# One gating tile issued ahead of the last gates and values, and the phasor table mirrored by GpSimd, in a two-layer streaming encoder

## The chip, the cores and the metric

The kernel runs on one core of one Trainium2 chip. Its engines are named as in the profile: PE (TensorE; PEld is its weight load), DVE (VectorE), ACT (ScalarE), POOL (GpSimd) and SP (SyncE, which here issues transfers only). ACT and SP both issue DMA transfers; ACTq and SPq stand for those instructions. The metric is the device time of one execution in microseconds (us), as the median of several runs.

## The reference

One inference step of a two-layer encoder, for 2,064 prompt tokens (16 of them meta tokens) and 128 sample tokens, 2,192 columns in all, in float32. The even layer, on which the change falls, computes:

```
def even_layer(h, g, i, st, P, segments):
    u = rmsnorm(h, g)
    ua, za, xb, zb = jnp.split(u @ P['ev_w_in'][i], [W_A, 2 * W_A, 2 * W_A + W_B], axis=-1)
    ya, s_re, s_im = s5_mixer(ua, ...)        # diagonal complex state space model, then a GLU: y * sigmoid(y @ w_glu)
    yb, mc, mn, mm, mbuf = mlstm_mixer(xb, ...)
    gated = jnp.concatenate([ya * jax.nn.silu(za), yb * jax.nn.silu(zb)], axis=-1)
    h = h + gated @ P['ev_w_out'][i]
```

In `mlstm_mixer`, a causal convolution over four tokens and a SiLU of `xb` give `xc`; `q` and `k` come from `xc` and `v` from `xb` by one matrix per head (four heads of 256); the input and forget gates are a product of `q`, `k`, `v` with `w_if`; a chunked recurrence follows. `zb` is the gating path. The odd layer (retention and an RG-LRU) is not touched by the change.

## The kernel before

Every float32 operand of a large product is split into a high and a low part (`split`, `narrow`), ACT casting the high part and POOL or DVE subtracting it for the low one; a product is then three TensorE instructions (`mm3`, L123 to L125). Tensors lie in SBUF with features on the 128 partitions and tokens along the row; tokens come in six blocks of up to 384 columns, and two blocks make a third.

The program is written phase by phase, and a scheduler of the Tile framework, which follows a simulated timeline, places each instruction on its engine's list, within the data dependences. Each engine runs its list strictly in that order. DMA transfers are issued in the order of the issuing engine's list.

Three phases matter here. In `phase_in0`, the S5 columns of the in-projection are made (`uas`, stored to `d_ua` by ACT at L305; `zst`, stored to `d_za` at L285). While the blocks run, `s5_turns` builds a table of phasors (powers of a rotation; `s5tb`, real and imaginary part, 128 partitions x 8 groups x 129 angles) for each of four groups of heads, one behind the other in the same piece of memory: DVE fills the upper 64 angles by doubling (L733 to L742, up to 128x256 elements per instruction), then the lower 64 are the upper ones in reverse order, times 1 for the real and -1 for the imaginary part (L744), and the table is stored to `d_rot` (L745, 1,032 KB). The next table may begin when the store has landed. At the end of the phase the first weights of the next phase (`w_first`: the load `xt`, the high part `wfh`, the low part `wfl`) are split into a place of memory that the tables give up.

`phase_l0` makes the mLSTM's input (`isz` 0) and its gating path (`isz` 1) third by third. `mtile(third, m, isz)` is one tile of 128 features: it loads a weight tile `wr`, splits it (`wh`, `wl`), multiplies it with the two blocks `ub` of the third (48 matmuls, into the PSUM tile `pm`), and for `isz` 0 does the convolution and yields what is late about it (the gate products `pg` of L428). `values` (L440 to L457) makes one head's `v` with its weights `wv`, `wvh`, `wvl` (36 matmuls of 264 columns for the six token tiles of a third). `settle(late)` runs the gate products and values still held back; `gate_out` writes the gates to memory (`d_g`, L516, L517), and the mLSTM's own opening reads them back (`g_i`, L1014). `s5` is a generator whose pieces are set between the tiles; behind its last products (the GLU, PSUM tile `s5p`, operands `s5gh`, `s5gl`) `phase_mlstm` follows (`pa` and `pc` tiles), whose first part is opened by `m_open` ahead of the gating tiles of the last third.

Of the kernel before, what the change touches and what calls it, by code (L numbers as in the profile page):

```python
# [13 lines left out]
OP = mybir.AluOpType  # L14
# [9 lines left out]
KD = 8  # L24
# [13 lines left out]
def P(e, name, bufs=1, side=None):  # L38
    return e.tc.tile_pool(name=name, bufs=bufs, side=side, reuse_waits="tile")
# [16 lines left out]
def cls(e, *names):  # L56
    for n in names:
        e.cms.pop(n).__exit__(None, None, None)
# [156 lines left out]
def phase_in0(e):  # L215
# [6 lines left out]
    with P(e, "a_w") as wp, P(e, "a_sb", 2) as sb, PS(e, "a_ps") as ps:  # L222
# [37 lines left out]
        for i, bi in enumerate(seq):  # L260
# [29 lines left out]
            if i == 1:  # L290
                with P(e, "prep", side="right") as rp:
                    prep_ml(e, rp, ps)
                s5_open(e, ps)
                s5_turns(e)
                cls(e, "s5pp")
# [59 lines left out]
def phase_l0(e):  # L355

    nc, tc = e.nc, e.tc
# [75 lines left out]
    def quarters(ut):  # L433

        n = sum(x[2] for x in ut) // 4
        return [(n * i, n) for i in range(4)]

    def values(h, ut, tiles, parts):

        h0 = ut[0][1]  # L440
        wv = xp.tile([128, 2, 264], F32, name="wv1", bufs=1)
        nc.sync.dma_start(wv[:, :, 0:256], e.i["ml_wv"][0, h].rearrange("(k p) f -> p k f", p=128))
        nc.gpsimd.tensor_copy(wv[:, :, 256:264], e.gw[:, 1, 2 * h:2 * h + 2, :])
        wvh = xp.tile([128, 2, 264], F32R, name="wvh1", bufs=1)
        wvl = xp.tile([128, 2, 264], F32R, name="wvl1", bufs=1)
        split(nc, wvh, wvl, wv, fine=True)
        for c, nt, kind, row in tiles:
            pv = ps.tile([128, 264], F32, name="pm1", bufs=4)
            cc = slice(c - h0, c - h0 + nt)
            for k in range(2):  # L450
                mm3(nc, pv[:nt], (parts[k][0][:, cc], parts[k][1][:, cc]), (wvh[:, k, :], wvl[:, k, :]), k == 0, k == 1)
            vo = xp.tile([128, 264], F32, name="vo1", bufs=3)
            nc.scalar.copy(vo[:nt], pv[:nt])  # L453
            nc.scalar.dma_start(e.v[c:c + nt, 256 * h:256 * (h + 1)], vo[:nt, 0:256])
            slot = 0 if kind == "x_sample" else 1 + tile_index(c)
            g = e.ga[:nt, :, slot, :]
            nc.gpsimd.tensor_add(g, g, vo[:nt, 256:264].rearrange("p (a b) -> p a b", a=2))  # L457
# [4 lines left out]
    def reload(bi):  # L462
        blk, b0, n = blks[bi]
        pool = e.ub_pool if bi % 3 < 2 else sb
        t = e.ub[bi] = pool.tile([128, 2, KD, 384], F32R, name=f"ub{bi % 3}", bufs=1)
        for c, nt, kind, row in blk:
            ur = xp.tile([128, KD, 128], F32, name="ut1", bufs=4)[:, :, :nt]
            nc.sync.dma_start(ur, e.u[:, :, c:c + nt])
            split(nc, t[:, 0, :, c - b0:c - b0 + nt], t[:, 1, :, c - b0:c - b0 + nt], ur)

    steps = 0
    for third in range(3):
        ut = [(bi,) + blks[bi][1:] for bi in (2 * third, 2 * third + 1)]
        tiles = blks[2 * third][0] + blks[2 * third + 1][0]
        pg = ps.tile([104, 192], F32, name="pg1", bufs=1)
        parts = []

        due, early, late = [], [], []
        if third > 0:

            early = [mtile(third, 0, 0, ut, pg, parts),
                     mtile(third, third % 2 == 0, third % 2, ut, pg, parts)]
            for g in early:
                next(g)
            reload(2 * third + 1)
            e.s5.loaded = third == 2

        def settle(held):

            for g in held:  # L490
                g()
            for h in due:
                values(h, ut, tiles, parts[2 * h:2 * h + 2])
            due.clear()

        def tile(m, isz):

            held = list(late)
            late.clear()
            for _ in early.pop(0) if early else mtile(third, m, isz, ut, pg, parts):  # L500
                pass
            settle(held)
            if m % 2 and not isz:
                due.append(m // 2)
            nonlocal steps
            steps += 1
            if steps == 1:
                cls(e, "w_first")
            if steps > 2:
                next(s5g, None)  # L510

        def gate_out():
            go = xp.tile([128, 2, 264], F32, name="wv1", bufs=1).rearrange("p a b -> p (a b)")
            for i, (o, n) in enumerate(quarters(ut)):
                g = slice(32 * i, 32 * i + 8)
                nc.scalar.activation(go[g, :n], pg[g, :n], AF.Identity, bias=bif[g])  # L516
                nc.scalar.dma_start(e.g8[:, ut[0][1] + o:ut[0][1] + o + n], go[g, :n])  # L517

        if third < 2:
            for m in range(KD):  # L520
                tile(m, 0)
                tile(m, 1)
                if m == 4:
                    reload(2 * third + 2)
            gate_out()
        else:
            for m in range(KD):
                tile(m, 0)
            for _ in s5g:
                pass  # L530
            settle(late)
            gate_out()
            co = xp.tile([128, D], F32, name="ut1", bufs=4)
            for g in range(2):
                pt = ps.tile([128, 512], F32, name="s5p", bufs=3)
                for m in range(4):
                    nc.tensor.transpose(pt[:27, 128 * m:128 * (m + 1)], cs[:, 4 * g + m, :], e.ident)
                nc.vector.tensor_copy(co[:27, 512 * g:512 * (g + 1)], pt[:27])
            nc.scalar.dma_start(e.o["p_ml_conv"].rearrange("a b c d -> (a b c) d"), co[0:3])
            nc.scalar.dma_start(e.o["s_ml_conv"].rearrange("a b c d -> (a b c) d"), co[3:27])  # L540
            cls(e, "b_x")
            m_open(e, ps)
            for m in range(KD):
                tile(m, 1)
    cls(e, "b_ps", "b_sb", "ub")

# [9 lines left out]
def cmul(v, o_re, o_im, a, b, s1, s2):  # L556
    v.tensor_mul(s1, a[0], b[0])
    v.tensor_mul(s2, a[1], b[1])
    v.tensor_sub(o_re, s1, s2)
    v.tensor_mul(s1, a[0], b[1])  # L560
    v.tensor_mul(s2, a[1], b[0])
    v.tensor_add(o_im, s1, s2)
# [122 lines left out]
MID = PCH // 2  # L685
# [37 lines left out]
def s5_turns(e):  # L723

    nc, v = e.nc, e.nc.vector
    p = e.s5
    with P(e, "s5co", side="right") as sb:
        for g0 in range(0, G, 8):
            gs = slice(g0, g0 + 8)
            tb = sb.tile([128, 2, 8, PCH], F32, name="s5tb")  # L730
            t1 = sb.tile([128, 8, 32], F32, name="s5r1")
            t2 = sb.tile([128, 8, 32], F32, name="s5r2")
            v.memset(tb[:, 0, :, MID], 1.0)  # L733
            v.memset(tb[:, 1, :, MID], 0.0)
            v.tensor_copy(tb[:, :, :, MID + 1], p.pp[:, :, 0, gs])
            for j in range(ROT):
                k = 1 << j
                sh = [128, 8, k]
                pk = [p.pp[:, i, j, gs, None].to_broadcast(sh) for i in range(2)]
                new, old = slice(MID + 1 + k, MID + 1 + 2 * k), slice(MID + 1, MID + 1 + k)  # L740
                cmul(v, tb[:, 0, :, new], tb[:, 1, :, new], (tb[:, 0, :, old], tb[:, 1, :, old]), pk,
                     t1[:, :, :k], t2[:, :, :k])  # L742
            for i in range(2):
                nc.scalar.mul(tb[:, i, :, 0:MID][:, :, ::-1], tb[:, i, :, MID + 1:], 1.0 - 2 * i)  # L744
            nc.scalar.dma_start(e.rot[:, :, gs, :], tb)  # L745


def s5_u(e, sb, q):
# [1310 lines left out]


PHASES = [phase_in0, phase_l0, phase_mlstm, phase_out0, phase_in1, phase_ret]


# [68 lines left out]
```

## Time and profile before

| what | value |
|---|---|
| time of three runs | 3120.72, 3131.16 and 3130.14 us, median 3130.14 us |
| the profiled execution's own time | 3125.61 us |
| its span, first to last instruction | 3123.9 us (1.7 us lie around it) |
| mean granted TensorE clock | 0.983 of full speed |
| busy over the span | PE 96%, DVE 55%, ACT 34%, POOL 31% |

All times of the trace are microseconds from the start of the span. PE's 4% of idle time is not spread evenly: one piece of it stands between 247 and 271 us, where `phase_in0` goes over into `phase_l0`.

### The profile page before, as it was taken

How to read it: one execution, taken by the hardware profiler on the slowest of the kernel's cores; microseconds unless marked ns; L12 is line 12 of the kernel's file. 1: busy time of each engine (PE TensorE's matmuls, PEld its weight loads, DVE VectorE, ACT ScalarE, POOL GpSimd, SP SyncE). 2: the span in 40 equal slices, each digit the busy share in tenths (PEclk: the TensorE clock that was granted, in tenths of full speed). 3: DMA queues.
4: the chain of work that ended last, by engine and by line, in shares of the span. 5: the costliest groups of instructions: out<-in, count | busy, mean ns of one | idle time of the engine just before them, and what ended most of it. 6: DMA issues, size and time to landing. Idle time of an engine off the chain costs nothing.

```text
span 3123.9 us, 45398 instructions
## 1 busy us (share of the span) xinstructions
PE 2995.7 (96%) x17435; PEld 2709.9 (87%) x17435; DVE 1717.8 (55%) x3482; ACT 1062.8 (34%) x1868; POOL 970.9 (31%) x1152
## 2 busy tenths in 40 slices
PE   8996999998999899999999999999999999999999
PEld 8996998997988887767799999999998898888887
DVE  4275885554547885233356666766610026665664
ACT  4223343335244433211235555555521112211221
POOL 6104664546436654111102111111100014433432
PEclk9998999998989999999999999999999999999999
DMA  6437555557634545665541111111122158544442
GB/s 214 120 100 210 158 168 151 164 165 159 209 91 149 171 153 171 212 196 169 152 147 59 48 49 52 51 52 52 43 84 75 52 157 249 140 127 131 135 124 75
DMA packets 447299, 404.82 MB, mean 130 GB/s; under 512 B 43593, under 2 KB 392977, under 8 KB 447082
## 3 DMA queue, kind: packets, MB, share of 16 engines
q1 hardware_dynamic: 335340, 272.36, 30.6%
q10 hardware_dynamic: 111742, 129.56, 12.4%
q8 instruction: 137, 2.24, 0.3%
q14 instruction: 80, 0.66, 0.1%
HBM read 266.35 MB, written 135.49 MB: 129 GB/s over the span
## 4 chain that ended last, share of the span: by engine, by line
PE 60%; DVE 8%; DMA 3%; issue 1%; ACT 1%; POOL 0%; SPq 0%; DVEq 0%; ACTq 0%; POOLq 0%
PE p_pm L124 8%; PE p_pm L125 8%; PE p_pm L123 8%; PE r_pm L125 4%; PE r_pm L124 4%; PE r_pm L123 4%; PE pa L123 3%; PE pa L124 3%; PE pa L125 3%; DVE p_d L1714 1%; PE pn L1363 1%; PE pc L1366 1%; DMA m_rw<-d_grow 1%; PE r_o L1916 1%; DVE m_qs L1206 1%
## 5 line engine op out<-in xcount | busy, mean ns | idle before, releaser
L123 PE MATMUL p_pm<-pu,p_wh 128*128 128x384 f32 (+1 forms) x1568 | 512.1, 327 | 0.2 <-ACT pu L105 0.2
L124 PE MATMUL p_pm<-pu,p_wh 128*128 128x384 f32 (+1 forms) x1568 | 511.8, 327 | 0.0
L125 PE MATMUL p_pm<-pu,p_wl 128*128 128x384 f32 (+1 forms) x1568 | 511.3, 326 | 0.0
L123 PE MATMUL pm<-ub,wh 128*128 128x384 f32 (+1 forms) x1136 | 378.6, 334 | 1.6 <-ACT vo L453 1.6
L124 PE MATMUL pm<-ub,wh 128*128 128x384 f32 (+1 forms) x1136 | 377.6, 332 | 1.6 <-DVE ub L109 1.6
L125 PE MATMUL pm<-ub,wl 128*128 128x384 f32 (+1 forms) x1136 | 375.2, 332 | 0.0
L123 PEld LDWEIGHTS p_pm<-pu,p_wh 128*128 128x128 f32 x1568 | 294.2, 188 | 1.8 <-issue 1.2
L124 PEld LDWEIGHTS p_pm<-pu,p_wh 128*128 128x128 f32 x1568 | 294.5, 188 | 1.0 <-issue 0.8
L125 PEld LDWEIGHTS p_pm<-pu,p_wl 128*128 128x128 f32 x1568 | 294.4, 188 | 0.0
L118 POOL TENSOR_TENSOR wl<-wr,wh 128x256 fp32r<-128x256 f32 x188 | 174.7, 959 | 222.4 <-ACT wh L105 222.4
L123 PEld LDWEIGHTS pm<-ub,wh 128*128 128x128 f32 x1136 | 216.3, 191 | 6.6 <-issue 4.0
L124 PEld LDWEIGHTS pm<-ub,wh 128*128 128x128 f32 x1136 | 216.3, 190 | 3.0 <-DVE ub L109 2.1
L124 PE MATMUL r_pm<-rol,r_gh 128*128 128x512 f32 x544 | 217.7, 401 | 1.1 <-POOL rol L109 0.6
L123 PE MATMUL r_pm<-roh,r_gh 128*128 128x512 f32 x544 | 217.9, 401 | 0.8 <-ACT p_o L1624 0.8
L125 PE MATMUL r_pm<-roh,r_gl 128*128 128x512 f32 x544 | 217.0, 400 | 0.7 <-DVE r_gl L109 0.7
L125 PEld LDWEIGHTS pm<-ub,wl 128*128 128x128 f32 x1136 | 215.9, 190 | 1.7 <-issue 1.6
L109 POOL TENSOR_TENSOR p_wl<-p_wr,p_wh 128x1024 fp32r<-128x1024 f32 x34 | 82.1, 2417 | 384.1 <-ACT p_wh L105 373.1
L109 POOL TENSOR_TENSOR p_xcl<-p_xc,p_xch 128x384 fp32r<-128x384 f32 (+1 forms) x48 | 46.8, 974 | 244.7 <-ACT p_xch L105 208.1
L125 PEld LDWEIGHTS r_pm<-roh,r_gl 128*128 128x128 f32 x544 | 102.9, 189 | 22.6 <-DVE r_gl L109 1.2
L124 PEld LDWEIGHTS r_pm<-rol,r_gh 128*128 128x128 f32 x544 | 102.9, 189 | 21.6 <-POOL rol L109 1.0
L123 PEld LDWEIGHTS r_pm<-roh,r_gh 128*128 128x128 f32 x544 | 102.7, 189 | 21.7 <-ACT p_o L1624 1.2
L1714 DVE RECIPROCAL p_d<-p_d 128x384 f32<-128x384 f32 (+1 forms) x48 | 116.7, 2430 | 0.6
(732 smaller groups left out, 6821.6 us busy)
## 6 DMA issues: line engine op xcount, KB each, us to landing
wr<-in_ev_w_in_dram SPq DMA_DIRECT2D x47, 512.0 KB
p_wr<-in_od_w_in_dram SPq DMA_DIRECT2D x40, 512.0 KB
d_in<-p_o ACTq DMA_DIRECT2D x80, 192.0 KB
m_rw<-d_grow SPq DMA_DIRECT2D x18, 512.0 KB
s5u<-d_ua SPq DMA_DIRECT2D x32, 274.0 KB
d_v<-vo ACTq DMA_DIRECT2D x68, 128.0 KB
m_va<-d_v SPq DMA_DIRECT2D x17, 512.0 KB
d_h<-o_x ACTq DMA_DIRECT2D x17, 512.0 KB
```

What stands on the lines that cost most here:

```text
L109: (nc.gpsimd if pool else nc.vector).tensor_tensor(l, x, h, op=OP.subtract)
L118: nc.gpsimd.tensor_tensor(out[:, c], a[:, c], b[:, c], op=op)
L123: nc.tensor.matmul(out, a[0], b[0], start=start, stop=False, **kw)
L124: nc.tensor.matmul(out, a[0], b[1], start=False, stop=False, **kw)
L125: nc.tensor.matmul(out, a[1], b[0], start=False, stop=stop, **kw)
L1206: v.tensor_tensor(qs[:, 4 * j:4 * j + 4, :n].rearrange("p (h m) n -> p h m n", m=2), qt[j][:, :, cs].rearrange("p (h m) n -> p h m n", m=2 ...
L1363: nc.tensor.matmul(pn[:n], c.qs[:, 2 * h + k, :n], ct[h][:, k, :], start=False, stop=k == 1)
L1366: nc.tensor.matmul(pc, c.kw[:n, h, 128 * k:128 * (k + 1)], c.va[:n, h, :], start=True, stop=True)
L1714: v.reciprocal(d[:, :n], d[:, :n])
L1916: nc.tensor.matmul(po, qk[:, h, :], S[:, h, :], start=False, stop=True)
```

## The change

Two edits. First, in the last third of `phase_l0`, the gating tile m = 0 is issued behind S5's last piece but ahead of `settle(late)` and `gate_out()`; the later loop starts at m = 1. Second, the mirror of the phasor table goes from ACT to POOL (with the reading side reversed instead of the writing side), and its store goes from ACT's list to SP's.

```
@@ phase_l0, third == 2
             for _ in s5g:
                 pass
+
+            for _ in mtile(third, 0, 1, ut, pg, parts):
+                pass
             settle(late)
             gate_out()
...
             m_open(e, ps)
-            for m in range(KD):
+            for m in range(1, KD):
                 tile(m, 1)
@@ s5_turns
             for i in range(2):
-                nc.scalar.mul(tb[:, i, :, 0:MID][:, :, ::-1], tb[:, i, :, MID + 1:], 1.0 - 2 * i)
-            nc.scalar.dma_start(e.rot[:, :, gs, :], tb)
+                nc.gpsimd.tensor_scalar(tb[:, i, :, 0:MID], tb[:, i, :, MID + 1:][:, :, ::-1], 1.0 - 2 * i, None,
+                                        op0=OP.mult)
+            nc.sync.dma_start(e.rot[:, :, gs, :], tb)
```

Each table has two mirror instructions of 128 x 8 x 64 elements and one store. In the changed file the mirror is L747 and the store L749.

POOL's list, where `phase_in0` ends and `phase_l0` begins (L185 and L186 are the last steps of the norm, `wl` and `wvl` the low parts of weights); before:

```order
L185 TENSOR_SCALAR rs_83<-rs_83 128x1
L186 TENSOR_TENSOR rs_83<-rs_83,mhalf 128x1
L408 MEMSET xb_2604 128x3
L443 COPY wv_2931<-gw 128x2x8
L118 TENSOR_TENSOR wl_2676<-wr_2673,wh_2675 128x256 x4
L118 TENSOR_TENSOR wl_2743<-wr_2740,wh_2742 128x256 x4
L118 TENSOR_TENSOR wvl_2935<-wv_2931,wvh_2934 128x264 x2
L443 COPY wv_3501<-gw 128x2x8
```

and of the change:

```order
L186 TENSOR_TENSOR rs_83<-rs_83,mhalf 128x1
L747 TENSOR_SCALAR s5tb<-s5tb 128x8x64 x6
L408 MEMSET xb_2604 128x3
L443 COPY wv_2931<-gw 128x2x8
L118 TENSOR_TENSOR wl_2676<-wr_2673,wh_2675 128x256 x4
L118 TENSOR_TENSOR wl_2743<-wr_2740,wh_2742 128x256 x4
L118 TENSOR_TENSOR wvl_2935<-wv_2931,wvh_2934 128x264 x2
L747 TENSOR_SCALAR s5tb<-s5tb 128x8x64 x2
L443 COPY wv_3501<-gw 128x2x8
```

The mirrors of the first three tables stand ahead of everything of `phase_l0`; the two of the fourth table stand behind ten splits of its weights.

SP's list at the same place (`bif` is the gates' bias, `ut` a block of the normed input read back); before:

```order
L300 DMA xt<-in_ev_w_in_dram 128x8x128
L368 DMA bif<-in_ml_b_if_dram 8x1 x4
L380 DMA wr_2673<-in_ev_w_in_dram 128x8x128
L380 DMA wr_2740<-in_ev_w_in_dram 128x8x128
L442 DMA wv_2931<-in_ml_wv_dram 128x2x256
```

and of the change:

```order
L300 DMA xt<-in_ev_w_in_dram 128x8x128
L749 DMA d_rot<-s5tb 256x1x1032 x3
L368 DMA bif<-in_ml_b_if_dram 8x1 x4
L380 DMA wr_2673<-in_ev_w_in_dram 128x8x128
L380 DMA wr_2740<-in_ev_w_in_dram 128x8x128
L442 DMA wv_2931<-in_ml_wv_dram 128x2x256
```

Three stores of tables now stand ahead of the loads of `phase_l0`. The fourth follows further on in the same list (`s5u` and `s5rt` are what S5 reads first):

```order
L468 DMA ut_4950<-d_u 128x8x128
L380 DMA wr_3057<-in_ev_w_in_dram 128x8x128
L468 DMA ut_4954<-d_u 128x8x128
L442 DMA wv_3501<-in_ml_wv_dram 128x2x256
L468 DMA ut_5951<-d_u 128x8x128
L749 DMA d_rot<-s5tb 256x1x1032
L757 DMA s5u<-d_ua 128x548 x2
```

It stands behind thirteen large loads of `phase_l0`, the last two of which are `wv_3501` (256 KB) and `ut_5951` (512 KB); before, no store of a table was on this list.

PE's list in the last third, where S5's GLU is under way (`pm_8190` is a value tile of head 3, `pm_8188` the gating tile m = 0, `pg` the gates); before:

```order
L428 MATMUL pg_6552<-xc_7605,gw 8x192 x4
L123 MATMUL pm_8190<-wvh_8185,xbh_7599 128x264
L124 MATMUL pm_8190<-wvl_8186,xbh_7599 128x264
L125 MATMUL pm_8190<-wvh_8185,xbl_7601 128x264
L123 MATMUL pm_8201<-wvh_8185,xbh_7599 128x264
```

and of the change at the same place:

```order
L428 MATMUL pg_6552<-xc_7605,gw 8x192 x4
L123 MATMUL pm_8188<-ub_5950,wh_8180 128x384
L124 MATMUL pm_8188<-ub_5950,wh_8180 128x384
L125 MATMUL pm_8188<-ub_5950,wl_8181 128x384
L123 MATMUL pm_8188<-ub_5950,wh_8180 128x384
```

The gating tile has taken the values' place. They now follow some 340 rows later on the same list, towards the end of the GLU:

```order
L125 MATMUL s5p<-s5gh,ut_6790 128x272
L428 MATMUL pg_6552<-xc_7858,gw 8x192 x2
L123 MATMUL pm_8253<-wvh_8248,xbh_7599 128x264
L124 MATMUL pm_8253<-wvl_8249,xbh_7599 128x264
L125 MATMUL pm_8253<-wvh_8248,xbl_7601 128x264
```

The last gates and the first value tile of head 3 stand here behind nearly all of the GLU's products.

## Rows read from the trace of the kernel before

**Rows 1.** The page: span, and busy time of each engine.

```profile
span 3123.9 us, 45398 instructions
PE 2995.7 (96%) x17435; PEld 2709.9 (87%) x17435; DVE 1717.8 (55%) x3482; ACT 1062.8 (34%) x1868; POOL 970.9 (31%) x1152
```

**Rows 2.** Waits between 180 and 320 us: total, times, longest.

```profile
POOL wl L118 <- ACT wh L105: 25.1, 4, 16.9
...
DVE s5tb L733 <- DMA d_rot<-s5tb: 31.7, 3, 14.9
...
PE pm L123 <- ACT wfh L105: 23.5, 1, 23.5
```

**Rows 3.** Windows: PE, PEld, DVE, ACT, POOL busy, clock, DMA share, GB/s.

```profile
247.00:270.50 23.50, 0.01 (x1) 0.00 (x0) 12.12 (x43) 9.88 (x14) 6.94 (x8) 0.59 1.02 311
...
785.00:826.00 41.00, 38.59 (x288) 37.29 (x287) 22.24 (x27) 13.78 (x35) 14.25 (x31) 1.00 0.45 150
826.00:888.00 62.00, 60.31 (x350) 58.88 (x347) 26.96 (x63) 17.42 (x27) 21.61 (x26) 1.00 0.74 221
888.00:937.00 49.00, 44.51 (x265) 35.05 (x266) 24.20 (x71) 24.94 (x56) 18.90 (x24) 0.83 0.23 67
```

**Rows 4.** Timeline of ACT, 238.5 to 270 us: start, duration, what, idle before.

```profile
239.23 6.55 ACTq L305 DMA_DIRECT2D d_ua<-uas  x8
...
245.85 1.70 ACTq L305 DMA_DIRECT2D d_ua<-uas  x2
247.59 1.16 ACT L744 ACTIVATE s5tb<-s5tb 128x512 f32<-128x512 f32 x2 [1.28 <-issue]
248.79 0.52 ACTq L745 DMA_DIRECT2D d_rot<-s5tb  x1
...
261.91 0.64 ACT L744 ACTIVATE s5tb<-s5tb 128x512 f32<-128x512 f32 x1 [11.30 <-DVE s5tb L559]
...
264.05 0.52 ACTq L745 DMA_DIRECT2D d_rot<-s5tb  x1
...
269.45 1.04 ACT L105 CAST wfh<-xt 128x1024 fp32r<-128x1024 f32 x1 [1.12 <-DMA d_rot<-s5tb]
```

**Rows 5.** Timeline of DVE, 222 to 272 us.

```profile
238.86 0.42 DVE L562 TENSOR_TENSOR s5tb<-s5r,s5r 128x256 f32<-128x256 f32 x1
254.14 0.07 DVE L733 MEMSET s5tb<- 128x8 f32 x1 [14.86 <-DMA d_rot<-s5tb]
...
262.71 0.42 DVE L562 TENSOR_TENSOR s5tb<-s5r,s5r 128x256 f32<-128x256 f32 x1
266.47 4.98 DVE L109 TENSOR_TENSOR ub<-ut,ub 128x1024 fp32r<-128x1024 f32 x3 [3.34 <-ACT ub L105]
```

**Rows 6.** Timeline of POOL, 240 to 312 us.

```profile
263.56 8.48 POOL L118 TENSOR_TENSOR wl<-wr,wh 128x256 fp32r<-128x256 f32 x8 [16.90 <-ACT wh L105]
272.00 3.42 POOL L118 TENSOR_TENSOR wvl<-wv,wvh 128x264 fp32r<-128x264 f32 x2
```

**Rows 7.** Timeline of SP (transfers issued), 240 to 285 us.

```profile
245.78 4.04 SPq L368 DMA_DIRECT2D bif<-in_ml_b_if_dram  x4
250.27 1.89 SPq L380 DMA_DIRECT2D wr<-in_ev_w_in_dram  x2
...
254.99 7.30 SPq L468 DMA_DIRECT2D ut<-d_u  x4
```

**Rows 8.** Tile `wr`, 240 to 300 us: its splits, shortest, median, longest in ns.

```profile
L118 POOL TENSOR_TENSOR wl<-wr,wh x16: 722/734/1720, 263.6 to 299.4; 128x256 fp32r<-128x256 f32 x16
```

**Rows 9.** POOL's groups by form: busy, mean ns, idle before.

```profile
L1222 POOL TENSOR_SCALAR_AFFINE_SELECT m_w<-m_w 128x512 f32<-128x512 f32 x17 | 14.3, 840 | 27.2 <-ACT m_w L1221 27.2
```

**Rows 10.** Waits of PE between 762 and 830 us.

```profile
PE s5p L123 <- DVE s5gy L991: 2.8, 3, 1.4
```

**Rows 11.** Tiles `g_i` (800 to 960 us) and `acol` (870 to 900 us).

```profile
L1014 SPq DMA_DIRECT2D g_i<-d_g x1: 265/265/265, 833.0 to 833.0; - x1
...
L1221 ACT ACTIVATE m_w<-m_rw,acol x8: 290/346/401, 894.8 to 899.1; 16x16 f32<-16x16 f32 x4, 128x128 f32<-128x128 f32 x4
```

## The prediction

> **What bounds the kernel now.** The page comes first [rows 1]: PE is busy for 96% of the span, DVE for 55%, and the rest is far below. So the kernel is PE's work plus the places where PE stands still, and a change that adds no matmul and removes none, as this one, can only move the 4% of idle time (about 128 us of 3123.9). Where these places are is read next. Both edits touch places that can be looked at by themselves: the tables are built until about 270 us, and the moved tile runs between 762 and 888 us.
>
> The waits between 180 and 320 us [rows 2] show one large stop of PE, 23.5 us, for the cast of `wfh`. In the windows [rows 3] the same stretch, 247 to 270.5, has PE at nothing while the DMA engines are full (share 1.02, 311 GB/s). Who ends it is read in the timeline of ACT [rows 4]: the cast of `wfh` starts at 269.45, released by the store of the fourth table, issued at 264.05 and landed 5.4 us later. That cast writes into memory which the tables give up, so PE's restart (269.45 + 1.04, and the first matmul at 270.55 by the waits' end) hangs on the fourth table, and this is a chain back: store issue 264.05, mirror from 261.91, DVE's table from 254.14 to 263.13 [rows 5], released by the landing of the third store, issued 248.79, its mirror at 247.59. The third table itself was ready at 239.28 [rows 5]; its mirror came 8.3 us late because ACT was issuing ten `d_ua` stores from 239.23 to 247.55 [rows 4]. So the chain to PE's restart runs through just the instructions that the second edit moves.
>
> The stretch around the first edit looks different [rows 3]: PE is busy for 38.6 of 41 us in 785 to 826 and 60.3 of 62 in 826 to 888. Between 762 and 830 it waits 2.8 us in all, three times, for S5's own DVE chain [rows 10].
>
> **Edit 1, the gating tile ahead of the last gates and values.** PE's work is the same in both orders: the tile's 48 matmuls of 384 columns, at 60.3 / 350 = 0.17 us each [rows 3] 8.3 us, go forward past 36 value matmuls and some gates. What it could gain is idle time that it fills: at most the 2.8 us of [rows 10], and these are waits in the middle of the GLU, which other ready matmuls already fill in part; the tile replaces the values as filling. What it could cost is that something behind the gates gets late: they go to `d_g`, which is read at 833.0, while the columns made from them are first used by ACT at 894.8 [rows 11]. The gates move back by some 8 us into this slack of 60 us, in which PE has gating tiles to run until 888 [rows 3]. I take nothing, with -3 and +3 as bounds (the waits of [rows 10] gone, or as much again). Without that cover, had the columns been needed at once, it would be up to the tile's 8.3 us. The scheduler also sets the recurrence's first matmuls anew; in 888 to 937 PE idles 4.5 us of 49 [rows 3], which such a shift can move by a few us either way.
>
> **Edit 2, third table.** On POOL, which idles here, the mirror can start when the table is ready, 239.3. The operation isn't in the trace. The nearest row is POOL's one-input instruction of the same 128x512, 0.84 us [rows 9]; a bound from below is ACT's 0.6 [rows 4], from above 0.84 stretched as POOL's splits stretch (1720 / 734 [rows 8]), 2.0. I take 0.84, so two end at 241.0. The store does not go at once: in the built program SP waits ahead of it for the completion of an earlier `d_ua` store, the same family that releases `bif` at 245.78 [rows 7]. I take 245.0 (241.0 to 248.8 as ends). Landing took 254.14 - 248.79 = 5.35, so the third table is stored at 250.4, a gain of 3.7 us.
>
> **Fourth table.** DVE needed 263.13 - 254.14 = 9.0; it ends at 259.4. Now POOL's list decides: its two mirrors stand behind ten splits of `phase_l0`'s first weights. These were held in [rows 2, 6] by ACT's cast (idle 16.9 us before 263.56), which stood behind ACT's mirror. With the mirror gone from ACT, the casts start when the weights land: issued 250.27 and 1.89 long for two [rows 7], 1.05 MB at the 311 GB/s of this stretch [rows 3] 3.4 us if it were alone, so about 254.5 beside other traffic, and a cast of 128x1024 takes 1.04 [rows 4]. Splits from 255.5 (253.5 to 257.5). They took 8.48 + 3.42 = 11.9 us for the ten [rows 6], while DVE did splits of its own [rows 5]; now DVE builds the table and then does those splits at the same time, so I keep 11.9: POOL is free at 267.4, 8 us after the table is ready. The bounds are ten at the median, 7.3, and ten at the longest, 17.2 [rows 8]. Mirrors to 269.1, store issue and landing 5.4 to 274.5, cast 1.04, and PE restarts at 275.5 to 275.6 instead of 270.55: **+5.0 us**. The fourth store's place on SP costs nothing if the loads ahead of it have been issued by 269. I take it that they have: the `ut` among them need buffers that DVE's splits give back, until 271.45 before [rows 5], and these splits follow a table that now ends 3.7 us sooner.
>
> Work that stands behind the mirror on POOL: small copies and the splits of the next tiles, which PE needs only after the restart. SP's first loads, behind three stores, go out as before, since the wait for `d_ua` held them until 245.78 already. PE pays the 5 us in full, as it has no other waits of size up to 320 [rows 2].
>
> Sum: 3125.6 + 5.0 + 0 = 3130.6 for an execution like the profiled one. The median of the runs shown is 4.5 above that execution, so the forecast is 3135 against 3130.1.
>
> **Rivals.**
> *The queue of SP.* The fourth store waits on SP's transfers behind `wv_3501` and `ut_5951` (0.77 MB, or 1.3 MB with the `ut` before them). For it: the DMA engines are full there (share 1.02). At 311 GB/s [rows 3] that is 2.5 to 4.2 us more, +7.5 to +9.2: 3138 to 3139. Against it: ACT's store shared the same full engines and landed in 5.4 us.
> The Trainium skill, page "DMA: Bandwidth & Descriptors", section "Queues, rings and completion order", says that SP and ACT each own a row of rings and that each DMA engine takes a row's descriptors in order and alternates between rows by packets. By that rule a store on ACT's row overtakes SP's loads and one on SP's row can't, which is this rival. No row of before shows a store on SP behind loads.
>
> *POOL is quick.* Splits at the median pace from 253.5 end at 260.8, mirrors 262.5, store 267.9, restart 269.0: -1.6, so 3128.5. For it: half of the splits take 0.73 or less [rows 8]. Against it: DVE is at work for most of those 7 us.
>
> *The tile fills the gaps.* All of the 2.8 us in [rows 10] and part of the 4.5 idle us at 888 to 937 disappear, edit 2 stays at the low end: 3126 to 3128.
>
> *Slow end.* DVE's two-operand table instructions hold POOL's two-operand splits down all the time: splits from 257.5 at 1.72 end at 274.7, mirrors at 2.0 each 278.7, store 284.1 and with 4 us of queue 288.1, restart 289.1, +18.6: 3149. It decides for slower by over 0.5% from 1.43 us a split with the other terms at their ends (257.5 + 14.3 + 4.0 + 5.4 + 4.0 + 1.04 = 286.2, against 270.55: +15.6).
> The Trainium skill, "GPSIMD Engine Reference", section "8. Key points", has GpSimd share its ports into SBUF with VectorE and contend with VectorE instructions of two SBUF inputs. The trace agrees for VectorE's 128x1024 splits: 0.73 us grew to as much as 1.72 beside them [rows 5, 8]; no row shows it for the table's small ones.
>
> *The opening moves the recurrence.* The scheduler's new order at 888 to 937 loses as much as that stretch idles now or more, 5 to 8 us: 3140 to 3143.
>
> **Chances and range.** Forecast (+2 to +7) 0.42; SP's queue 0.20; quick POOL 0.13; gaps filled 0.09; slow end 0.07; recurrence 0.09. 0.5%, about what a measurement of this kernel can tell from no change, is 15.6 us. Nothing here gives 15.6 us less (two thirds of the 23.5 us stop would have to go), so faster gets 0.04. Slower takes the slow end and mishaps together, 0.09; same 0.87. The runs of before differ by 10 us among themselves, which goes into the range: from 3121 (quick POOL and a low run) to 3147 (close to the slow end).
>
> **What would show it.** In the profile after: the first mirrors on POOL at about 239 to 241 and the third store issued near 245; the fourth table's end on DVE near 259.4; ten splits on POOL from 255 to 267 with the mirrors directly behind; PE's wait for `wfh` 28.5 us instead of 23.5. If the wait is under 23, the splits were quick or the third store went far earlier. If the store's landing takes 8 us or more, it is SP's queue. If PE's idle time in 762 to 937 changes by over 3 us, edit 1 is not the zero that I take. The forecast is wrong if PE's restart is between these bounds and the time is not: then something outside of both places moved.

## The result and the profile after

The change made the kernel slower: 3143.82 us as the median of four runs, against 3128.39 for the kernel before beside them, a ratio of 1.0051 (95% interval 1.0034 to 1.0067), or +15.4 us. The forecast was 3135 with a range of 3121 to 3147. The sign was the one forecast. Of the 15.4 us, 9.6 came at the place and along the chain that were forecast, about twice the +5.0 of the sum; the rest came in a later stage that the sum had put at nothing. One run of `e12_two_more` below, 3546 us at a granted clock of 0.784, was in a slower state of the chip and is left out of its median.

The page of the changed kernel, first lines: PE does the same work as before [rows 1], 2992.6 us of it, in a span that is 18.6 us longer than that of the profile before.

```profile
span 3142.5 us, 45397 instructions
PE 2992.6 (95%) x17435; PEld 2706.5 (86%) x17435; DVE 1717.0 (55%) x3482; ACT 1058.5 (34%) x1860; POOL 982.4 (31%) x1160
```

The waits between 180 and 340 us (total, times, longest). PE's stop for `wfh` has grown from 23.5 [rows 2] to 34.1 us, and the cast itself now waits 13.3 us for the store of the table; before, it waited 1.12 [rows 4].

```profile
POOL s5tb L747 <- DVE s5tb L562: 66.9, 3, 34.9
...
PE pm L123 <- ACT wfh L105: 34.1, 1, 34.1
POOL wl L118 <- ACT wh L105: 28.2, 5, 13.5
...
ACT wfh L105 <- DMA d_rot<-s5tb: 13.3, 1, 13.3
...
DVE xd L415 <- DMA bif<-in_ml_b_if_dram: 10.5, 1, 10.5
```

The timeline of POOL over the same stretch shows the fourth table's mirrors where its list has them: behind ten splits, and 3.92 us long. The earlier pairs, in front of which POOL idles, take 3.14 to 3.15 us. The last line is the view of the tile `s5tb` on POOL: shortest, median and longest of the eight mirrors in ns. The shortest is the fourth table's second one, which no work of DVE overlaps; the longest is its first one, which runs beside a split of DVE's (`ub`, 1.76 us from 268.45). The first mirror of the three earlier pairs runs beside the last steps of DVE's table and takes 1.67 to 1.68 us.

```profile
202.62 3.15 POOL L747 TENSOR_SCALAR s5tb<-s5tb 128x512 f32<-128x512 f32 x2 [34.91 <-DVE s5tb L562]
...
240.86 3.14 POOL L747 TENSOR_SCALAR s5tb<-s5tb 128x512 f32<-128x512 f32 x2 [19.06 <-DVE s5tb L562]
...
259.05 6.71 POOL L118 TENSOR_TENSOR wl<-wr,wh 128x256 fp32r<-128x256 f32 x8 [13.51 <-ACT wh L105]
265.72 3.40 POOL L118 TENSOR_TENSOR wvl<-wv,wvh 128x264 fp32r<-128x264 f32 x2
269.10 3.92 POOL L747 TENSOR_SCALAR s5tb<-s5tb 128x512 f32<-128x512 f32 x2
...
L747 POOL TENSOR_SCALAR s5tb<-s5tb x8: 1488/1586/2465, 202.6 to 271.5; 128x512 f32<-128x512 f32 x8
```

The timeline of SP (transfers issued), of two stretches. The third store goes at 244.03 instead of 248.79, the fourth at 273.05 instead of 264.05 [rows 4].

```profile
244.03 0.51 SPq L749 DMA_DIRECT2D d_rot<-s5tb  x1
244.63 7.29 SPq L368 DMA_DIRECT2D bif<-in_ml_b_if_dram  x4
252.66 1.40 SPq L380 DMA_DIRECT2D wr<-in_ev_w_in_dram  x2
...
273.05 0.56 SPq L749 DMA_DIRECT2D d_rot<-s5tb  x1
```

The timeline of ACT. The cast of the first weight, which waits for its landing, starts only at 257.93, and the cast of `wfh` ends at 280.05, where PE starts again (280.11).

```profile
245.34 4.17 ACTq L305 DMA_DIRECT2D d_ua<-uas  x2
...
257.93 1.04 ACT L105 CAST wh<-wr 128x1024 fp32r<-128x1024 f32 x1 [7.11 <-DMA wr<-in_ev_w_in_dram]
...
279.01 1.04 ACT L105 CAST wfh<-xt 128x1024 fp32r<-128x1024 f32 x1 [13.28 <-DMA d_rot<-s5tb]
```

The timeline of DVE. The fourth table begins at 253.07, only 1.1 us earlier than before [rows 5], because a small copy (`xd`) now stands ahead of it on DVE's list and waits for transfers; and it ends at 265.2, 12.1 us later instead of 9.0. Its steps of 128x256, 0.42 us before [rows 5], take 0.83 to 0.95 while POOL splits beside them.

```profile
252.93 0.18 DVE L415 COPY xd<-pc 128x24 f32<-128x24 f32 x1 [10.54 <-DMA bif<-in_ml_b_if_dram]
253.07 0.07 DVE L736 MEMSET s5tb<- 128x8 f32 x1
...
264.35 0.83 DVE L565 TENSOR_TENSOR s5tb<-s5r,s5r 128x256 f32<-128x256 f32 x1
```

So the restart moved from 270.55 to 280.11, by 9.6 us. That leaves about 6 of the 15.4 us in the medians, and 9 of the 18.6 in the profiles, for something behind it.

### The profile page after: what moved, and what is told of

It is laid out like the page before. It is cut to its first block, busy times and chain, and to the rows that moved or that the text cites. A ratio compares the mean times of both kernels' runs of the same rounds, so it can differ in the third digit from the quotient of the medians.

```text
span 3142.5 us, 45397 instructions
## 1 busy us (share of the span) xinstructions
PE 2992.6 (95%) x17435; PEld 2706.5 (86%) x17435; DVE 1717.0 (55%) x3482; ACT 1058.5 (34%) x1860; POOL 982.4 (31%) x1160
## 4 chain that ended last, share of the span: by engine, by line
PE 61%; DVE 8%; DMA 2%; issue 1%; ACT 1%; POOL 1%; SPq 0%; ACTq 0%; DVEq 0%; POOLq 0%
PE p_pm L124 8%; PE p_pm L125 8%; PE p_pm L123 8%; PE r_pm L124 4%; PE r_pm L125 4%; PE r_pm L123 4%; PE pa L123 3%; PE pa L124 3%; PE pa L125 3%; PE pn L1367 1%; PE pc L1370 1%; DVE p_d L1718 1%; PE pa L1235 1%; DMA m_rw<-d_grow 1%; DVE p_xc L554 1%
```

## The experiments

Theory A was that the restart is all of it, theory B that the first edit adds something behind it, theory C that the stores on SP's list do the damage. Theory D came after the first runs: the scheduler writes a different list for the mLSTM's recurrence, far behind the edit. Each kernel was timed beside the kernel before on the same chip; "restart" is PE's first matmul with `wfh` in its profile, and "list" says how PE's list of the recurrence, as the traces have it, stands to that of before (apart from the tile that the first edit moves).

| kernel | edit | median and difference, us | ratio, 95% | restart, us | list |
|---|---|---|---|---|---|
| the change | both | 3143.82, +15.4 | 1.0034 to 1.0067 | 280.1 | as e2_table |
| e1_tile | first edit alone | 3124.22, -3.8 | 0.9978 to 1.0002 | 270.3 | before, but for 63 rows near its end |
| e2_table | second edit alone | 3142.09, +14.1 | 1.0033 to 1.0061 | 281.4 | other, some 600 rows |
| e3_pool_actq | mirror on POOL, store on ACT | 3142.40, +15.8 | 1.0041 to 1.0066 | 279.0 | as e2_table |
| e4_act_spq | mirror on ACT, store on SP | 3128.27, +0.2 | 0.9991 to 1.0009 | 271.6 | before |
| e5_dve_spq | mirror on DVE, store on SP | 3128.11, +0.2 | 0.9994 to 1.0011 | 270.5 | before |
| e7_hybrid | fourth table as before | 3132.11, +4.2 | 1.0000 to 1.0025 | 273.5 | before, but for some 110 rows near its end |
| e8_order | 3 mirrors more on ACT | 3138.99, +11.1 | 1.0021 to 1.0047 | 274.5 | as e2_table |
| e9_late | 28 mirrors more on ACT | 3144.93, +17.0 | 1.0043 to 1.0067 | 289.8 | before |
| e10_three_dve | DVE, fourth on ACT | 3130.38, +3.7 | 1.0000 to 1.0019 | 269.2 | before |
| e11_three_dve_tile | the same and first edit | 3124.78, -1.9 | 0.9984 to 1.0003 | 270.9 | as e1_tile |
| e12_two_more | e2_table, 2 mirrors more | 3138.25, +11.1 | 1.0021 to 1.0047 | 282.0 | as e1_tile |

**e0_before**, the kernel before unchanged, for a second profile of it.

> The kernel before, unchanged, as a second profile of it. Theory A (the time beyond PE's restart is a gather that runs at a different pace from one execution to the next): the last of the four activations on s5gy starts some 16 us after the first in the profile of before and 30.4 us in that of the change; here the figure lies anywhere between, and the span moves with it by up to 5 us against 3123.9. Theory B (the slower gather belongs to the change): the figure is 24.8 us as in the profile of before (741.99 - 717.23 = 24.8), and the span within 2 us of 3123.9.

Its span is 3127.6 us, its restart 270.7. The timeline of ACT has the four activations on S5's gathered output:

```profile
717.78 2.04 ACT L953 ACTIVATE s5gy<-s5gy 128x2192 f32<-128x2192 f32 x1
...
729.36 2.03 ACT L953 ACTIVATE s5gy<-s5gy 128x2192 f32<-128x2192 f32 x1 [7.19 <-DMA s5gy<-d_ys]
...
747.20 2.03 ACT L953 ACTIVATE s5gy<-s5gy 128x2192 f32<-128x2192 f32 x1
```

From first to last 29.4 us, where the first profile of the same kernel had 24.8 and the change's has 30.4. (The expectation's "16 us" for the first profile is a slip; 24.8, further on in it, is the figure.) So some 5 us of the difference between the two first profiles is this gather, which takes another time in another execution; the profile of before was an unusually quick one there. The comparisons below use e0_before.

**e1_tile and e2_table**, the two edits apart.

```
e1_tile   + for _ in mtile(third, 0, 1, ut, pg, parts): pass        (ahead of settle(late); later loop from 1)
e2_table  - nc.scalar.mul(...)         + nc.gpsimd.tensor_scalar(...)
          - nc.scalar.dma_start(...)   + nc.sync.dma_start(...)
```

> The first edit alone. Theory A (all of the loss is in the table's chain to PE's restart): restart near 270.5 us as before, time -3 to +2 us against the kernel before. Theory B (the moved tile changes loads and reads around S5's gather and costs the 5 to 6 us that the trace of the change loses between 700 and 762 us): restart near 270.5, but +3 to +6 us.

> The second edit alone. Theory A: PE's wait for wfh is 34 us and its restart at 280 us as in the changed kernel, +9 to +16 us against the kernel before, that is the whole of the change's loss. Theory B: restart at 280, +9 to +10 us and no more, the rest being the first edit's.

The second edit alone gives +14.1 us, the whole of the change's loss within the intervals; theory B fell. The first edit alone measured -3.8 us, in an interval (-6.9 to +0.6) that includes zero. But e2_table's restart is 10.8 us late, and theory A as it stood does not say where the rest went.

**e4_act_spq and e3_pool_actq**, one half of the second edit each.

```
e4_act_spq     mirror: nc.scalar.mul          store: nc.sync.dma_start
e3_pool_actq   mirror: nc.gpsimd.tensor_scalar  store: nc.scalar.dma_start
```

> The mirror stays on ACT, only the store goes to SP's list. Theory A (GpSimd's place behind ten splits and its 1.6 us per mirror make the restart late, the store's list does not): the fourth mirror at about 262, the fourth store right behind it (its place on SP's list is here ahead of the last input loads), restart at 269 to 272, time -3 to +3 us. Theory C (stores on SP's list delay the weight loads and collide with the last S5 stores, and this is what costs): wr issued at 252.5 instead of 250.3 us, restart 274 or later, +4 us or more.

> The second edit with the store left on ACT's list; the mirror on GpSimd. Theory A (GpSimd's mirrors, their place and price): the fourth mirrors again end at 270 to 273 us, the store lands 5.4 us later, restart at 278 to 281, and the recurrence has the second edit's list: +11 to +15 us. Theory C (the stores on SP's list hold up the loads): wr issued at 250 instead of 252.6, splits 2.5 us sooner, restart at 276 to 277, +9 us or less.

In the time, the store's list costs nothing that can be measured, and the mirror on POOL costs everything: theory C fell. (At the restart the store's list does show in one of them: in e2_table the store is issued at 272.76, 1.7 us behind its mirrors, because `wv` and `ut` stand ahead of it on SP's list, and lands 7.56 us later; in e3_pool_actq it goes at once and lands in 6.83, and the restart is 2.4 us sooner.) In e3_pool_actq `wr` was issued at 250.29 and not at 252.66, and yet the first cast of it, the first sign that it has landed, began at 257.80, as late as in the change:

```profile
257.80 1.04 ACT L105 CAST wh<-wr 128x1024 fp32r<-128x1024 f32 x1 [8.58 <-DMA wr<-in_ev_w_in_dram]
...
271.10 0.52 ACTq L746 DMA_DIRECT2D d_rot<-s5tb  x1
277.93 1.04 ACT L105 CAST wfh<-xt 128x1024 fp32r<-128x1024 f32 x1 [11.71 <-DMA d_rot<-s5tb]
```

**e7_hybrid**: POOL and SP for three tables, the fourth as before on ACT.

```
+ if g0 < 24: nc.gpsimd.tensor_scalar(...)   else: nc.scalar.mul(...)
+ (nc.sync if g0 < 24 else nc.scalar).dma_start(...)
```

> The second edit for the first three tables; the fourth keeps ACT for its mirror and its store. Theory A (what costs is the fourth mirror's place on GpSimd, behind ten splits, and its 2 us a piece there): table four ends at 262 to 263 as in the change, ACT's mirror by 264.5, store landed at 270, restart at 271 to 272, +0 to +2 us. Theory C (the three stores on SP's list cost): restart at 276 or later, +5 us or more.

Restart 273.5, 7.9 us sooner than e2_table's: the fourth table's mirror on POOL carries most of the late restart. What is left over the kernel before is seen on DVE: the fourth table began at 253.42 and its last step is this, with the mirror right behind it on ACT at 266.59:

```profile
253.42 0.07 DVE L733 MEMSET s5tb<- 128x8 f32 x1
...
265.71 0.84 DVE L562 TENSOR_TENSOR s5tb<-s5r,s5r 128x256 f32<-128x256 f32 x1
```

13.1 us for a table that took 9.0 [rows 5]: with ACT's casts no longer behind a mirror, POOL's splits start while the table is being made and hold DVE up.

**e8_order and e9_late**, the restart and the recurrence's list apart. A few mirrors more on ACT (they write the same values again) are enough for the scheduler to write PE's list of the recurrence exactly as e2_table has it; with 28 more, PE's list is exactly that of before.

```
e8_order   - for i in range(2):    + for i in [1] * (3 if g0 == 24 else 0) + [0, 1]:
e9_late    - for i in range(2):    + for i in [0, 1] * (15 if g0 == 24 else 1):
```

> The kernel before, with the second mirror of the fourth table done three times more on ACT. The restart is late by some 2 us (3 x 0.63), and this is enough that the scheduler writes PE's list of the mLSTM's recurrence, far behind, in just the order that it has with the second edit. Theory D (the loss behind the restart, some 4 us in the medians, is this other order): +5 to +7 us. Theory A (only the restart counts): +1.5 to +2.5 us.

> The kernel before, with the fourth table's mirrors done 28 times more on ACT; PE's list, the recurrence included, is the same as before. The restart is late by 17 to 18 us (28 x 0.63). If a late restart is paid in full and no more (theories A and D): +16 to +19 us. If what follows recovers some of it: less; if a late restart by itself makes later stages slower, as the second edit's +14 for a restart 10 us late could mean: +22 us or more.

e9_late is late by 19 us at the restart and costs 17.0: a late restart is paid about once, no more. e8_order is late by 4 us (not 2) and costs 11.1. So the list costs some 7 us in this pair of medians (2.7 to 10.8 by the interval), more than theory D expected. The waits of PE between 890 and 1270 us show it. In e0_before they sum to 33.0 us in ten rows, the first of which are:

```profile
PE pa L123 <- DVE m_g L1272: 17.3, 5, 3.5
PE pc L1366 <- DVE ct L1370: 4.6, 3, 1.8
PE pa L1269 <- DVE m_g L1272: 3.9, 2, 3.5
```

In e8_order 36.8 us in twelve rows, with a new one, for `m_yn`:

```profile
PE pa L123 <- DVE m_g L1272: 13.9, 4, 3.5
PE pc L1366 <- DVE ct L1370: 7.1, 4, 2.6
PE pa L1269 <- DVE m_g L1272: 4.4, 3, 3.5
PE pn L1361 <- ACT m_yn L1256: 3.9, 3, 1.6
```

And in the changed kernel 38.8 us, with the same pattern:

```profile
PE pa L123 <- DVE m_g L1276: 13.9, 4, 3.5
PE pc L1370 <- DVE ct L1374: 7.3, 5, 2.6
PE pn L1365 <- ACT m_yn L1260: 4.9, 3, 2.2
```

The windows of the whole stage, from the last matmul of `phase_l0`'s gating tiles to the first of the output projection, say the same. In order: e0_before, e5_dve_spq and e10_three_dve with the list of before, then e8_order and the change with the other (length; PE, PEld, DVE, ACT, POOL busy; clock; DMA share; GB/s).

```profile
893.00:1206.50 313.50, 280.40 (x1624) 241.56 (x1623) 246.74 (x732) 130.81 (x273) 177.92 (x215) 0.92 0.47 143
894.10:1203.00 308.90, 275.76 (x1623) 236.91 (x1623) 247.59 (x732) 130.60 (x273) 178.26 (x215) 0.94 0.47 145
889.70:1207.40 317.70, 282.48 (x1623) 243.75 (x1623) 246.30 (x732) 130.40 (x273) 177.08 (x215) 0.92 0.47 141
894.80:1213.50 318.70, 281.80 (x1623) 241.33 (x1623) 238.63 (x727) 129.55 (x272) 174.91 (x213) 0.93 0.45 137
900.00:1219.50 319.50, 280.53 (x1623) 241.02 (x1623) 238.69 (x726) 129.29 (x272) 174.69 (x213) 0.94 0.45 137
```

PE is idle for 33.1, 33.1 and 35.2 us in the first three, for 36.9 and 39.0 in the last two. Over all profiles the four kernels with the other list have 36.9 to 39.0 us, all the rest 32.2 to 35.2, and e9_late, with the latest restart, 33.1. So the order itself is worth 4 to 6 us of PE's idle time. The length of the stage is a weaker sign: PE's busy time for the same matmuls differs by 7 us between two executions with one list (275.8 at a granted clock of 0.94, 282.5 at 0.92).

**e12_two_more**: e2_table with the fourth table's second mirror done twice more on POOL, with which the list comes out almost as before.

```
- for i in range(2):    + for i in [1] * (2 if g0 == 24 else 0) + [0, 1]:
```

> The second edit, with the fourth table's second mirror done twice more on GpSimd. The restart is 3 to 4 us later still, at 284 to 285 us, but the scheduler's list of the recurrence is, but for eight short pieces near its end, that of before. Theory D (the second edit's list costs some 4 us behind the restart): +12 to +14 us, no more than the second edit alone. Theory A' (a restart late by 10 us costs 14 whatever the list): +17 to +18 us.

More work on the path, and 11.1 us lost instead of 14.1, about as much as the restart is late (11.4). The restart was less late than expected, because the store left right behind the last mirror and landed in 5.94 us, where e2_table's was held as said above; and two intervals of this width (6.6 to 14.7 and 10 to 19 us) overlap, so this run alone would decide little; the waits, 34.0 us without the row for `m_yn`, go with it.

**e5_dve_spq, e10_three_dve and e11_three_dve_tile**, versions that might beat both.

```
e5_dve_spq      v.tensor_scalar(...), nc.sync.dma_start(...) for all four tables
e10_three_dve   the same for three, nc.scalar.mul and nc.scalar.dma_start for the fourth
e11_three_dve_tile   e10_three_dve and the first edit
```

> The mirror on DVE, right behind each table, the store on SP's list (ahead of the last input loads); PE's list is that of before. A mirror of 128x512 is not in the trace for DVE; 0.3 to 0.6 us from its 0.42 for 128x256 with two inputs. Theory A: third store at about 244, table four from about 250 to 260, its store at 260 to 261, restart at 267 to 268, that is 2.5 to 3.5 us earlier than before: -2 to -4 us. Theory C (an early third store holds up the last S5 stores and with them everything on SP): restart at 271 or later, no gain.

> The first three tables' mirrors on DVE with their stores on SP's list, the fourth's on ACT ahead of the casts of the weights, with its store on ACT's list; PE's list is that of before. Theory A: the third store lands at 250 to 251 and table four, with no GpSimd split beside it, takes 9.0 us to 260; mirror on ACT to 261.3, store 262.4 (a cast stands between), landed 267.8, restart at 268.9, some 2 us earlier than before: -1 to -3 us. Theory C (an early third store costs as much as it gives): restart at 270.5 to 272, 0 to +2 us.

> The same with the first edit, and the recurrence's list as the first edit alone has it: the sum of the two, -4 to -8 us, if they do not touch each other; if the first edit's 4 us were chance, -1 to -3 us.

On DVE the mirror takes 0.42 us, and in e5_dve_spq the third table's second one was done at 237.5; its store still had to wait for the S5 stores. In e5_dve_spq the splits on POOL began at 258.38, beside the table, and the last mirror ended at 263.7; nothing was gained. In e10_three_dve the mirror on ACT stands ahead of the casts, the splits begin at 262.68, and the table is undisturbed; its last step:

```profile
251.75 0.07 DVE L733 MEMSET s5tb<- 128x8 f32 x1 [14.09 <-DMA d_rot<-s5tb]
...
260.57 0.43 DVE L562 TENSOR_TENSOR s5tb<-s5r,s5r 128x256 f32<-128x256 f32 x1
```

9.2 us, and the restart came 1.5 us sooner. But the time is +3.7 us (0 to +5.9), which the restart does not explain. Its profile has the excess in the recurrence, 4.2 us over e0_before's with the same list (2.1 idle, 2.1 busy, by the windows above); the cause is open. No version here is measurably faster than the kernel before; e1_tile and e11_three_dve_tile come nearest.

## Why the prediction was right in kind and too small

The measured time lies in the stated range, but the central case (+2 to +7, chance 0.42) did not come: the measured interval is +10.6 to +21. That 3143.8 lies under the 3147 is in part luck. The upper end was set for POOL's splits at their slowest; what filled it was a chain twice as late as summed, for other reasons, and a loss in the recurrence. Nor was 15.6 us the smallest change that can be told from none: the interval here is some 5 us to either side.

**The chain to the restart** was read rightly: third store early, fourth mirrors behind ten splits, store, cast, restart. It gave +5.0; +9.6 was measured. Its terms:

| term | taken | measured in the change |
|---|---|---|
| third store issued | 245.0 | 244.0 |
| fourth table begins, takes | 250.4, 9.0 | 253.1, 12.1 |
| splits begin | 255.5 | 259.05 |
| ten splits | 11.9 | 10.05 |
| two mirrors | 1.7 | 3.92 |
| issue to landing | 5.4 | 5.96 |
| restart | 275.5 | 280.1 |

The step "the casts start when the weights land ... so about 254.5" failed first, by 3.4 us, and the splits began at 259.05, beyond the text's own 253.5 to 257.5. It set the 1.05 MB of the two weights against the rate, with 0.8 us for the company they have: the trace of before has a `d_rot` store (1,032 KB, issued 248.79) and a `d_za` store (768 KB, 250.64) ahead of and beside them, together 2.85 MB, which at the 311 GB/s of [rows 3] from 248.8 would end at 258 (an estimate). In e3_pool_actq the transfers stand like that, and the first cast starts at 257.80. In the change the `d_rot` store went 4.8 us sooner, but then the last S5 stores (`d_ua`, issued until 249.5 instead of 247.55) came later, and with them `bif` and `wr` on SP, and the first cast was as late. No run tested this account by itself. The profile of before could not show it, because ACT stood behind its mirror and looked for the weights later.

The step "The nearest row is POOL's one-input instruction of the same 128x512, 0.84 us" was the second: the mirror takes 1.49 us alone and 1.58 to 2.47 beside work of DVE's. For the pair, 3.92 us, the bound of 2.0 a piece held; the middle did not. What in this instruction costs nearly twice the other (the reversed read, or the operation) was not tried. In the other direction went the ten splits, 10.05 us for 11.9, because eight of them ran beside the table and only two beside DVE's long splits. And the loads ahead of the fourth store were issued by 270.8 and not by 269, which cost nothing here, as the mirrors ended only at 273.0.

No run put the fourth mirrors ahead of the splits on POOL's list. How their place and their price share the delay is read from the timeline alone: the table is done at 265.2, the splits hold POOL until 269.1, and the mirrors take until 273.0.

The third table's gain of 3.7 us came to nothing much, for two reasons that the text did not see: the copy `xd` that the scheduler set ahead of the fourth table on DVE, and the contention that stretched it. Neither was on the path, since POOL reached the mirrors only at 269.1, after the table's end at 265.2; but with the mirror on another engine (e7_hybrid) it would be next.

**Edit 1 at nothing**, bounds -3 to +3: measured -3.8, not distinguishable from nothing. The waits for S5's chain are 2.8 us [rows 10] before and 2.1 to 3.4 in the other kernels without the edit, 1.9 in the change and 1.7 in e1_tile, so the tile may fill about 1 us. The rest of that run's gain is open: its list of the recurrence is the same as that of e12_two_more, which gained nothing behind its restart.

**The recurrence** is the term that the sum set to zero and that measured some 6 us. The text had it as a rival ("The scheduler's new order at 888 to 937", 5 to 8 us, chance 0.09), and its size came; but the text tied it to the first edit and to the stretch next to that. It is the second edit that does it, from some 700 us away, and the new waits for `m_yn` lie between 990 and 1040. Taking the late restart (against 270.6) off the median's difference leaves 5.9, 3.3, 7.4 and 7.2 us for the four kernels with the other list (the change, e2_table, e3_pool_actq, e8_order), and -0.8, 0.3, -2.2 and 5.1 us for those with the list of before (e4_act_spq, e5_dve_spq, e9_late, e10_three_dve); 1.3, -0.3, -3.5 and -2.2 for those that differ only near its end (e7_hybrid, e12_two_more, e1_tile, e11_three_dve_tile). Each of these figures has an interval of some 3 to 5 us to either side. That the list is the cause rests on PE's idle time in the stage, which parts the two groups without an exception, and on e8_order, which has little else. In the medians e10_three_dve does not fit, and what it lost is not explained.

**The rivals.** SP's queue: the fourth store landed 5.96 us after issue behind its loads, 0.6 more than the text took and not 2.5 to 4.2. By the rule of the Trainium skill, "DMA: Bandwidth & Descriptors", section "Queues, rings and completion order", each DMA engine consumes the descriptors of a row in order, so a store starts behind those ahead of it in its own row. The trace agrees that loads were still under way: the first of the store's packets of 4,128 bytes starts 2.25 us after the issue, and 1.18 in e9_late, where nothing else moves. But on ACT's row in e3_pool_actq it starts after 3.16 us, so the row alone does not decide. Roughly, the landing goes with the bytes moved until then, the store's own included: 1.06 MB in 4.35 us (e9_late, ACT), 2.34 in 5.96 (the change, SP), 2.55 in 6.83 (e3_pool_actq, ACT), 2.87 in 7.56 (e2_table, SP); e11_three_dve_tile (ACT), 2.31 in 7.14, is slower than that.

Quick POOL: the ten splits took 10.05 and not 7.3; 8.2 in e2_table, e7_hybrid and e12_two_more came nearest. The slow end did not come: POOL's splits of 128x256 took 0.77 to 0.91 us beside the table's steps, 0.72 to 0.73 with nothing beside them and 1.7 only beside DVE's splits of 128x1024. It was the table that was held up: the trace shows DVE's table steps at 0.83 to 0.95 us beside POOL's splits and at 0.42 without them. That is what the Trainium skill, "GPSIMD Engine Reference", section "8. Key points", says of two engines that share their ports into SBUF, and here the small steps show it too.

## What to carry to other kernels

An instruction moved to an idle engine is not served when its input is ready, but when that engine's list comes to it: read the list between, and price the path by the splits that stand ahead. When several transfers meet on full DMA engines, add all their bytes before dividing by the rate. And where a scheduler works from a simulated timeline, a shift of a few microseconds early on can rewrite a stage far behind; compare the lists of all stages, and time a version that has the list alone.

## What was not expected of the hardware

The mirror of 128x512 takes 1.49 us on POOL with nothing beside it and 1.58 to 2.47 beside DVE, 0.64 on ACT, and on DVE 0.42 alone and 0.83 to 0.95 beside POOL's splits (e5_dve_spq). DVE's two-input steps of 128x256 double, from 0.42 to 0.83 to 0.95 us, while POOL splits run, so a table of 9.0 us became one of 12.1 to 13.1 us. And the gather of S5's output took 24.8 and 29.4 us in two executions of one kernel, and 24.8 is the shortest of the fourteen profiles here (26.5 to 30.4 in the others). The difference is a third of the change's whole effect: one profile of each kernel would have put it down to the change.
